# Two-layer hybrid attention encoder on one core: modulation as dot products along the free axis, and an opening in two halves of the rows

## The chip, the cores and the metric

The kernel runs on one core of a Trainium2 chip. A core has five engines with instruction queues of their own: TensorE (PE, which multiplies a 128x128 stationary operand by a moving operand of up to 512 columns), VectorE (DVE), ScalarE (ACT), GpSimd (POOL) and SyncE (SP, which here issues the transfers). They meet at semaphores. The metric is the device time of one execution in microseconds.

## The reference, cut to what matters

```python
c_act = silu(c)                                   # [1, 1024]
for i in range(2):
    mod = c_act @ ada_w[i] + ada_b[i]             # 1024 x 3072
    shift, scale, gate = split(mod, 3)
    h = rms_norm(x, norm_g[i]) * (1 + scale) + shift
    out = layer_ab(h, ...) if i == 0 else layer_diff(h, ...)
    x = x + gate * out
return rms_norm(x, final_g)

def layer_ab(h, pos, w_in, ...):
    cq, ckv, kr, q_sb, k_sb, v_sb, z = split(h @ w_in, ...)   # 384, 256, 32, 512, 512, 512, 1024
    q = rms_norm(cq, q_norm_g) @ w_uq             # rope on a part of q
    kv = rms_norm(ckv, kv_norm_g) @ w_ukv
    k_rope = rope(kr, pos)                        # one key for all heads
    ...                                           # latent attention, stick-breaking attention
    return (concat(o_mla, o_sb) * silu(z)) @ w_out
```

There are 1024 rows of 1024 features. The change touches the modulation (`mod`) and the first products of layer 0: the latents `cq` and `ckv`, the key `kr` and four of the eight blocks of `z`.

## The kernel before, in words

Every product is done in three passes (`mm3`, L172 to L175): each operand is split into a rounded part and the rest (`hi` and `lo`), and PE runs hi x hi, hi x lo and lo x hi into one bank of PSUM. A block is 128 columns of the weights; over 1024 rows and 1024 features it takes 8 x 3 matmuls of 128x512 for each half of the rows. Weights come as 0.5 MB (`w_st`); ACT rounds them (`w_hi`, L159) and POOL or DVE takes the rest (`w_lo`, L154), in `wprep`. All transfers are issued in order by SP (`dma`, L80).

The opening of layer 0 (L496 to L706) works so. All eight tiles of x are loaded, squared (ACT L526, DVE L523) and scaled by their inverse norms (`rstd_cols`, then L532 and L534). `ada_block(k)` (L538) makes the shift and scale of 128 features: `ada_st` holds 1 MB of `ada_w` with the summed index on the partitions; DVE multiplies eight pieces of 128x256 by a column of `c_act` and adds them up (L542, L544), and PE sums over the partitions with matmuls of one column (L547). PE transposes the rows (L554, two groups of four 128x128), ACT applies scale and shift (`hf`, L239) and rounds (`h0h`), and POOL or, for the first and last k, DVE takes the rest (`h0l`, L154). The three blocks of `cq` run over k, as the features come, for both halves of the rows. Then follow, each over all its k in turn (`dense_fm`): the two blocks of `ckv`, the block of `kr`, and four blocks of `z`.

Beside these stand: the rotary table `cs` (DVE L653 to L661, then the sine on ACT, L662), with a buffer of its own (tag "cs"); the rotated key, made from the banks of `kr` by a DVE multiply with `cs` (`krt`, L642), four copies on ACT (`krc`, L693) and an add on POOL; the row tables `te` and `to` (L681 to L686); and the rest of the modulation, for both gates and layer 1 (`ada_rest`, L590): two sweeps over 2048 columns, each 32 DVE operations of 128x512 (L478, L480) on 8 MB, and 16 one-column sums on PE (L487). `more(n)` hands out its steps between the blocks. Banks: `s_bank` gives three (`sc`), `d_bank` two (`psd`), `v_bank` one (`pv`), `t_bank` two (`tr`). After the opening the stick-breaking heads begin with a product into `psd`.

The order on each engine is set by a scheduler when the kernel is built, from the order of the code and from `issue_after`; at run time every engine works its queue strictly in that order.

Of the kernel before, what the change touches and what calls it, by code (L numbers as in the profile page):

```python
# [28 lines left out]
ORDER = (4, 0, 5, 1, 6, 2, 7, 3)      # by chunk parity, small beside large  # L29
ORDER_SEQ = (0, 1, 4, 2, 3, 5, 6, 7)  # first half of the tokens first  # L30
# [42 lines left out]
def kernel(ctx, tc, a, out):  # L73
# [33 lines left out]
    # scratch in DRAM  # L107
# [19 lines left out]
    # constants  # L127
# [49 lines left out]
    def dense_fm(w, rhs, evac, bank=None):  # L177
        """feature-major rows of one block of 128 columns, in two halves of the tokens"""
# [9 lines left out]
    def rstd_cols(pool, ss, n, scale, eps, name, extra=None, bufs=2):  # L188
        """(scale * ss + eps * extra) ** -0.5 of [P, n] columns"""
# [16 lines left out]
    def row_out(pool, cols, n, dst, bank):  # L206
        """[P, n] columns (query in block, block) to rows of n blocks in DRAM"""
# [6 lines left out]
    def row_bc(src, n):  # L214
        """a row in DRAM, on n partitions"""
# [5 lines left out]
    def cols_bc(dg, cols, bank):  # L221
        """four columns [P, 4] (query in block, block) as rows on every partition, in a bank"""
# [7 lines left out]
    def row_sums(tile_of, nt, bank):  # L230
        """sums over the partitions of tile_of(t), as columns [P, nt]"""
# [14 lines left out]
    def z_evac(z, func, scale):  # L246
        """z * sigmoid(z), or twice that from tanh(z / 2)"""
# [16 lines left out]
    def v_rows(vs, hi, lo, n):  # L264
        """token-major halves of the values in vs; hi(g), lo(g) of four token tiles"""
# [95 lines left out]
    def qk_dense(w, hT, b_t, bank=None):  # L361
        """[qh;qh], [ql;0], [kh;kl] of one head whose weights are [q | k]"""
# [21 lines left out]
    def par_view(ap, par, seq=False):  # L384
        """the tokens of chunks par and 2 + par; with seq of chunks 2 par and 2 par + 1"""
# [26 lines left out]
    def finish_half(pool, pv, par, e, ot, seq=False):  # L412
        """add the two halves ([vh|vl] or [vl|vh]) of a bank holding the chunks of par_view"""
# [7 lines left out]
    def load_wo(layer, half, f2s, alloc, gate, eng):  # L421
        """feature blocks 2 f2, 2 f2 + 1 of one half of the columns, times the gate, split"""
# [34 lines left out]
    def out_half(ys, wo, fs, x_, xr, bank):  # L457
        """x_ = xr + rows of y times columns of wo"""
# [35 lines left out]
    X_TAGS = [("lsq0", 1), ("lsq1", 1), ("lsq2", 1), ("zb", 2), ("zb", 2), ("lat_h", 2), ("lat_h", 2), ("lat_l", 2)]  # L494

    # =====================================================================  # L496
    # layer 0: modulation, transposed rows, latents
    # =====================================================================
    hT = [(res(f"h0h{k}"), res(f"h0l{k}")) for k in range(KC)]
    with tc.tile_pool(name="a0", bufs=1, reuse_waits="tile") as a0:  # L500
        sgc = a0.tile([P, 8], F32, name="sgc")
        nc.scalar.activation(sgc, c_sb, AF.Sigmoid)
        nc.vector.tensor_mul(c_act, c_sb, sgc)
# [10 lines left out]
        for g in range(2):  # L514
# [20 lines left out]
            if g == 0:  # L535
                ada_load(0)
# [671 lines left out]
```

## Time and profile before

| | |
|---|---|
| median of 3 runs | 1489.6 us (1489.22 to 1493.49) |
| span of the profiled execution | 1489.6 us |
| PE busy, whole span | 1394.9 us (94%) |
| DVE, ACT, POOL busy | 956.8 us (64%), 670.5 us (45%), 446.2 us (30%) |
| PE busy in the first 50 us | 6.14 us of 30, then 14.24 us of 20 |
| PE busy from 50 to 125 us | all of it |

The profiled execution is the median of the runs. A share of busy time is an average over the whole span; the opening is a small part of it, in which PE first waits for the loads, then for DVE and ACT, and from 50 us on runs almost without a gap.

### The profile page before, as it was taken

How to read it: one execution, taken by the hardware profiler on the slowest of the kernel's cores; microseconds unless marked ns; L12 is line 12 of the kernel's file. 1: busy time of each engine (PE TensorE's matmuls, PEld its weight loads, DVE VectorE, ACT ScalarE, POOL GpSimd, SP SyncE). 2: the span in 40 equal slices, each digit the busy share in tenths (PEclk: the TensorE clock that was granted, in tenths of full speed). 3: DMA queues.
4: the chain of work that ended last, by engine and by line, in shares of the span. 5: the costliest groups of instructions: out<-in, count | busy, mean ns of one | idle time of the engine just before them, and what ended most of it. 6: DMA issues, size and time to landing. Idle time of an engine off the chain costs nothing.

```text
span 1489.6 us, 20993 instructions
## 1 busy us (share of the span) xinstructions
PE 1394.9 (94%) x7328; PEld 1160.7 (78%) x7328; DVE 956.8 (64%) x2155; ACT 670.5 (45%) x1368; POOL 446.2 (30%) x509
## 2 busy tenths in 40 slices
PE   3899999999998899999879899999999999997797
PEld 2777888888886688887767688888888888886686
DVE  7769637667779865576557526665565756567674
ACT  4452145555556653555345324444444535354321
POOL 1534221132427354635133321133121222134100
PEclk9999999999999999999989999999999999999899
DMA  9269522131224166433747131324232324346262
GB/s 375 67 261 382 206 77 75 49 90 50 75 69 186 36 188 213 136 123 100 215 136 268 29 108 48 86 85 114 71 100 64 92 64 114 78 111 179 82 201 93
DMA packets 109640, 189.85 MB, mean 127 GB/s; under 512 B 8736, under 2 KB 70040, under 8 KB 107488
## 3 DMA queue, kind: packets, MB, share of 16 engines
q1 hardware_dynamic: 109536, 188.53, 39.9%
q8 instruction: 58, 0.95, 0.3%
q14 instruction: 46, 0.38, 0.1%
HBM read 131.23 MB, written 39.27 MB: 114 GB/s over the span
## 4 chain that ended last, share of the span: by engine, by line
PE 40%; DVE 5%; DMA 4%; issue 1%; POOL 1%; ACT 1%; SPq 0%; DVEq 0%; ACTq 0%; POOLq 0%
PE psd L173 8%; PE psd L175 8%; PE psd L174 8%; PE sc L294 4%; PE pv L328 3%; PE sc L173 2%; PE sc L174 2%; PE sc L175 2%; DMA y_hi<-yh_d 1%; DMA w_st<-in_wo_dram 1%; PE pv L234 1%; PE tr L308 1%; PE tr L309 1%; PE tr L310 1%; DVE g L1029 1%
## 5 line engine op out<-in xcount | busy, mean ns | idle before, releaser
L154 POOL TENSOR_TENSOR w_lo<-w_st,w_hi 128x1024 fp32r<-128x1024 f32 (+2 forms) x63 | 153.6, 2440 | 370.7 <-ACT w_hi L159 370.4
L154 DVE TENSOR_TENSOR pt_l<-tr,pt_h 128x512 fp32r<-128x512 f32 (+1 forms) x240 | 148.8, 630 | 104.9 <-ACT pt_h L159 97.4
L159 ACT CAST pt_h<-tr 128x512 fp32r<-128x512 f32 (+1 forms) x240 | 126.2, 547 | 147.0 <-PE tr L310 136.1
L175 PE MATMUL psd<-h1h,w_lo 128*128 128x512 f32 x448 | 177.0, 395 | 0.0
L174 PE MATMUL psd<-h1l,w_hi 128*128 128x512 f32 x448 | 176.2, 393 | 0.0
L173 PE MATMUL psd<-h1h,w_hi 128*128 128x512 f32 x448 | 176.1, 393 | 0.0
L294 PE MATMUL sc<-qk_k,qk_a 128*128 128x512 f32 (+2 forms) x288 | 104.8, 369 | 3.6 <-ACT g L747 1.3
L173 PE MATMUL psd<-h0h,w_hi 128*128 128x512 f32 x264 | 106.7, 404 | 0.0
L174 PE MATMUL psd<-h0l,w_hi 128*128 128x512 f32 x264 | 105.6, 400 | 0.0
L175 PE MATMUL psd<-h0h,w_lo 128*128 128x512 f32 x264 | 105.2, 398 | 0.0
L294 PE MATMUL sc<-qk_k,qk_b 128*128 128x512 f32 (+2 forms) x288 | 98.5, 349 | 0.0
L1029 DVE CUSTOM_DVE_ANT_0 g<-sc,tz 128x512 f32<-128x512 f32 (+3 forms) x128 | 72.1, 585 | 40.1 <-PE sc L294 33.7
L159 ACT CAST w_hi<-w_st 128x1024 fp32r<-128x1024 f32 x56 | 58.9, 1052 | 86.4 <-PE sc L174 36.2
L174 PEld LDWEIGHTS psd<-h1l,w_hi 128*128 128x128 f32 x448 | 84.2, 188 | 17.1
L175 PEld LDWEIGHTS psd<-h1h,w_lo 128*128 128x128 f32 x448 | 84.2, 188 | 16.1
L173 PEld LDWEIGHTS psd<-h1h,w_hi 128*128 128x128 f32 x448 | 84.2, 188 | 16.1
L328 PE MATMUL pv<-pt_l,vt 128*128 128x256 f32 x320 | 88.7, 303 | 8.2 <-DVE pt_l L154 7.4
L1035 ACT ACTIVATE g<-g,st 128x640 f32<-128x640 f32 (+3 forms) x64 | 63.4, 990 | 67.8 <-DVE st L1034 63.1
L328 PE MATMUL pv<-pt_h,vt 128*128 128x256 f32 x320 | 89.5, 296 | 3.3 <-POOL pt_h L314 1.7
L749 DVE TENSOR_TENSOR_SCAN g<-g 128x640 f32<-128x640 f32 (+3 forms) x32 | 68.7, 2148 | 14.7 <-ACT g L746 14.6
L328 PEld LDWEIGHTS pv<-pt_l,vt 128*128 128x128 f32 x320 | 62.0, 194 | 12.0 <-issue 4.7
L328 PEld LDWEIGHTS pv<-pt_h,vt 128*128 128x128 f32 x320 | 61.8, 193 | 9.5 <-DVE ot L418 2.7
(469 smaller groups left out, 3743.3 us busy)
## 6 DMA issues: line engine op xcount, KB each, us to landing
w_st<-in_w_dram SPq DMA_DIRECT2D x46, 512.0 KB
ada_st<-in_ada_k_dram SPq DMA_DIRECT2D x8, 1024.0 KB
ada_st<-in_ada_w_dram SPq DMA_DIRECT2D x16, 512.0 KB
ada_st<-in_ada_w_dram SPq DMA_DIRECT2D x8, 1024.0 KB
w_st<-in_wo_dram SPq DMA_DIRECT2D x16, 512.0 KB
yh_d<-yh SPq DMA_DIRECT2D x28, 256.0 KB
yl_d<-yl SPq DMA_DIRECT2D x28, 256.0 KB
w_st<-in_wv_dram SPq DMA_DIRECT2D x12, 512.0 KB
```

What stands on the lines that cost most here:

```text
L154: return (nc.vector if eng == "vec" else nc.gpsimd).tensor_tensor(out_, x_, y_, op=ALU.subtract)
L159: nc.scalar.copy(hi, src)
L173: mm(ps, sh, mh, start=start, stop=False)
L174: mm(ps, sh, ml, start=False, stop=False)
L175: mm(ps, sl, mh, start=False, stop=stop)
L234: mm(ps[:, t:t + 1], tile_of(t), ones, start=True, stop=True)
L294: mm(ps[:, :nn], st[:, q], mv[:, lo_:lo_ + nn], start=m == 0, stop=not diag and m == len(pairs) - 1)
L308: nc.tensor.transpose(tr[:, P:256], pb[:, (2 * j + 1) * P:(2 * j + 2) * P], identf)
L328: mm(dst, st, tt[w][:, m * 256:m * 256 + 256], start=j == 0 and m == 0 and x == 0, stop=j == n - 1 and m == 1 and x == len(ps_) - 1)
L749: nc.vector.tensor_tensor_scan(ur, ur, ur, 1.0, op0=ALU.mult, op1=ALU.bypass)
L1029: nc.vector.tensor_tensor_reduce(e_[:, sl], ps, tz[:, S - L + sl.start:S - L + sl.stop], op0=ALU.add, op1=ALU.max, scale=1.0, scalar=-3e38 ...
L1035: nc.scalar.activation(e_[:, :L], e_[:, :L], AF.Exp, scale=0.125, bias=st[:, 2 + c:3 + c], accum_out=lst[:, c1:c1 + 1] if c == 0 else st[: ...
```

## The change

- The rows are worked in two halves of 512. x tiles 0 to 3 are loaded first; x tiles 4 to 7 come after the fourth piece of `ada_w` and are normalised while the first half is multiplied. All squares are on ACT, one scaling of each half on DVE (`SC`).
- The features' scale and shift are dot products along the free axis: the pieces of `ada_w` now lie with the feature on the partition (`ada_t`, `ada_r`: prepared in this layout with the inputs), and `c`, copied to all partitions and passed through silu (`cb`), is the other operand. `dots` does two DVE operations of 128x1024 for 1 MB. Only the first 128 features are done on PE, with 16 matmuls of one column whose stationary operand is the piece of `ada_w` (`ada_0`).
- `ada_rest` uses the same dots on sixteen pieces of 1 MB; there are no sums over partitions on PE any more. The gates' row is written at the end.
- The weights of all five latent blocks (three `cq`, two `ckv`) are loaded and split at the front (`w_load`; the rest of three of them on DVE, of two on POOL), some in buffers that later hold x. The five blocks of the first half run over k in five banks; the second half follows.
- `h0l` is always made by DVE.
- Norms of the latents are added in halves (POOL, 128x512). Weights of `kr` and of the four z blocks may be fetched once the last of the eight modulation pieces is under way.
- `cb` is allocated with the tag "cs".

```diff
-WLO = ("vec", "pool")
+SC = "aava"
+WLO = ("vec", "vec", "vec", "pool", "pool")
...
+        cb = a0.tile([P, D], F32, name="cb", tag="cs")
+        dma(cb, a["c"].to_broadcast([P, D]))
+        csg = a0.tile([P, D], F32, name="csg", tag="junkd")
+        nc.scalar.activation(csg, cb, AF.Sigmoid)
+        nc.vector.tensor_mul(cb, cb, csg)
...
+            ada_st[k] = a0.tile([P, 2, D], F32, name="ada_st", tag="ld", bufs=NLD)
+            return dma(ada_st[k].rearrange("p i d -> p (i d)"), a["ada_t"][k - 1] if k else a["ada_0"])
...
+            m = a0.tile([P, 2], F32, name="adm", tag="adm", bufs=4)
+            for n in range(2):
+                junk = a0.tile([P, D], F32, name="junkd", tag="junkd")
+                nc.vector.tensor_tensor_reduce(junk, st[:, n, :], cb, op0=ALU.mult, op1=ALU.add, scale=1.0, scalar=0.0,
+                                               accum_out=m[:, n:n + 1])
+            return m
...
-            ac = a0.tile([P, 256], F32, name="ack", tag="ack", bufs=2)
-            nc.vector.tensor_scalar(ac, st[:, 0, :], c_act[:, 0:1], None, op0=ALU.mult)
-            for r in range(1, KC):
-                nc.vector.scalar_tensor_tensor(ac, st[:, r, :], c_act[:, r:r + 1], ac, op0=ALU.mult, op1=ALU.add)
-            ps = t_bank()
-            for n in range(2):
-                mm(ps[:, n:n + 1], ac[:, n * P:n * P + P], ones, start=True, stop=True)
-            nc.vector.tensor_tensor(modc[0][:, k::8], ps[:, 0:2], adab[:, k:16:8], op=ALU.add)
-            nc.vector.scalar_tensor_tensor(gsc[0][:, k:k + 1], modc[0][:, 8 + k:9 + k], 1.0, ng[:, k:k + 1],
-                                           op0=ALU.add, op1=ALU.mult)
...
+            m = dots(ada_st[k]) if k else a0_ps
+            nc.vector.tensor_tensor(modc[0][:, k::8], m, adab[:, k:16:8], op=ALU.add)
+            return nc.vector.scalar_tensor_tensor(gsc[0][:, k:k + 1], modc[0][:, 8 + k:9 + k], 1.0, ng[:, k:k + 1],
+                                                  op0=ALU.add, op1=ALU.mult)
...
+        x0 = x_load(0)
+        ada_load(0)
+        a0_ps = v_bank()[:, 0:2]
+        st0 = ada_st[0].rearrange("p i d -> p (i d)").rearrange("p (k i c) -> p k i c", i=2, c=P)
+        for n in range(2):
+            for k in range(KC):
+                mm(a0_ps[:, n:n + 1], st0[:, k, n, :], c_act[:, k:k + 1], start=k == 0, stop=k == KC - 1)
+        normed = x_norm(x0)
+        with tc.issue_after(normed.ins):
+            known = ada_block(0)
+            x_mod(0, 0, x0, "vec")
+            with tc.issue_after(known.ins):
+                for b in (0, 1):
+                    w_load(b)
+                ada_load(1)
+                for b in (2, 3):
+                    w_load(b)
+                ada_load(2)
+                w_load(4)
+        loaded = ada_load(3)
+        with tc.issue_after(loaded.ins):
+            x1 = x_load(1)
+        fb = [s_bank(), s_bank(), s_bank(), d_bank(), d_bank()]
...
+                known = ada_block(k + 1)
+                _, done = x_mod(0, k + 1, x0, "vec")
+                if k + 4 < KC:
+                    held = ada_load(k + 4)
+            if k == 2:
+                with tc.issue_after(known.ins), tc.issue_after(done.ins):
+                    x_norm(x1)
+            for b in range(5):
+                mm3(fb[b], wl[b][0][:, k, :], wl[b][1][:, k, :], hT[k][0][:, :512], hT[k][1][:, :512], k == 0, k == KC - 1)
...
+        for k in range(KC):
+            ready, _ = x_mod(1, k, x1, "vec")
+        for b in range(5):
+            latent_evac(b, 0, fb[b])
+        for b in range(5):
+            ps = (s_bank, d_bank)[b % 2]()
+            for k in range(KC):
+                mm3(ps, wl[b][0][:, k, :], wl[b][1][:, k, :], hT[k][0][:, 512:], hT[k][1][:, 512:], k == 0, k == KC - 1)
+            latent_evac(b, 1, ps)
...
+            cs = a0.tile([P, S], F32, name="cs", tag="cs")
...
+            nc.scalar.activation(cs, ar, AF.Sin, scale=cst[:, 3:4])
...
-                yield from ada_sweep(a0, src if n == 0 else lambda st, r: dma(st, a["ada_w"][1, r, 0:2048]), acc)
...
+                dst, b_ = ((gt, bias[:, 2::3, :]), (modc[1], bias[:, 3:5, :]))[n]
+                dst = dst.rearrange("p (i n) -> p i n", n=8)
+                for k in range(KC):
+                    st = a0.tile([P, 2, D], F32, name="ada_st", tag="ld", bufs=NLD)
+                    dma(st.rearrange("p i d -> p (i d)"), a["ada_r"][n, k])
+                    nc.vector.tensor_tensor(dst[:, :, k], dots(st), b_[:, :, k], op=ALU.add)
+                    yield k
...
+            part = lambda half, b: sqt[half, b // 2][:, b % 2 * 512:b % 2 * 512 + 512]
+            for half in range(2):
+                for b in range(b0 + 1, b0 + n):
+                    nc.gpsimd.tensor_tensor(part(half, b0), part(half, b0), part(half, b), op=ALU.add)
+            ss = row_sums(lambda t: part(t // 4, b0)[:, t % 4 * P:t % 4 * P + P], NT, v_bank)
...
+        with tc.issue_after(held.ins):
+            wkr = wprep(a["w0"][21])
+        dense_fm(wkr, hT, kr_evac, s_bank)
...
-            z = a0.tile([P, S], F32, name="zb", tag="zb", bufs=2)
-            dense_fm(wprep(a["w0"][8 + 4 + b]), hT, z_evac(z, AF.Sigmoid, 1.0), s_bank)
+            z = wide("zb", "a")
+            with tc.issue_after(held.ins):
+                wz = wprep(a["w0"][8 + 4 + b])
+            dense_fm(wz, hT, z_evac(z, AF.Sigmoid, 1.0), s_bank)
             dma(zs_d[b], z)
             more(4)
         more(16)
+        row_out(a0, gt, 16, gate_d.rearrange("i (n p) -> (i n) p", p=P), t_bank)
```

The order changes at three places that matter below. The first is ACT after the latents, where it makes the rotary table. Before (`lsq`, `lat_h`: squares and splits of the latents; `krc`: the copies of the rotated key; `zb`: the activation of z):

```order
L620 ACTIVATE lsq<-sc 128x512
L621 ACTIVATE lat_h<-sc,smalls 128x512
L620 ACTIVATE lsq<-sc 128x512
L621 ACTIVATE lat_h<-sc,smalls 128x512
L159 CAST w_hi<-w_st 128x1024
L620 ACTIVATE lsq<-sc 128x512
L621 ACTIVATE lat_h<-sc,smalls 128x512
L662 ACT_TABLE_LOAD
L662 ACTIVATE cs<-ar,smalls 128x1024
L159 CAST w_hi<-w_st 128x1024
L693 COPY krc<-krt 32x1024 x4
L249 ACT_TABLE_LOAD
L249 ACTIVATE zb<-sc 128x512
L159 CAST w_hi<-w_st 128x1024
L249 ACTIVATE zb<-sc 128x512 x2
```

Now:

```order
L604 ACTIVATE lat_h<-sc,smalls 128x512
L601 ACTIVATE lsq<-psd 128x512
L604 ACTIVATE lat_h<-psd,smalls 128x512
L601 ACTIVATE lsq<-sc 128x512
L604 ACTIVATE lat_h<-sc,smalls 128x512
L661 ACTIVATE rows<-tr 8x384 x3
L158 CAST w_hi<-w_st 128x1024
L637 ACT_TABLE_LOAD
L637 ACTIVATE cs<-ar,smalls 128x1024
L248 ACT_TABLE_LOAD
L248 ACTIVATE zb<-sc 128x512
L718 COPY krc<-krt 32x1024 x4
L158 CAST w_hi<-w_st 128x1024
L248 ACTIVATE zb<-sc 128x512 x2
```

The table `cs` stands behind the splits of the latents and ahead of the first `zb` and the copies in both; the weight that was rounded between the table and the copies is now rounded ahead of the table. In the changed kernel the activation that writes `cs` waits for the last reader of `cb`, whose buffer it takes; that reader is the last of the 32 dots of `ada_rest`, the second of the pair in the next listing.

The second place is DVE at the end of `ada_rest` and the rotated key. Before, where `krt` is made (`rlt`, `rlr`: steps of an inverse norm; `acc`: the sweep; `lat_l`: the rest of a latent):

```order
L622 SCALAR_TENSOR_TENSOR lat_l<-sc,smalls,lat_h 128x512
L480 SCALAR_TENSOR_TENSOR acc<-ada_st,c_act,acc 128x512
L203 SCALAR_TENSOR_TENSOR rlr<-rlt,rlr 128x8
L480 SCALAR_TENSOR_TENSOR acc<-ada_st,c_act,acc 128x512 x4
L201 TENSOR_TENSOR rlt<-rlr 128x8
L480 SCALAR_TENSOR_TENSOR acc<-ada_st,c_act,acc 128x512
L642 TENSOR_TENSOR krt<-sc,cs 128x512
L480 SCALAR_TENSOR_TENSOR acc<-ada_st,c_act,acc 128x512
L202 TENSOR_TENSOR rlt<-rlt,rlh 128x8
L642 TENSOR_TENSOR krt<-sc,cs 128x512
L203 SCALAR_TENSOR_TENSOR rlr<-rlt,rlr 128x8
L201 TENSOR_TENSOR rlt<-rlr 128x8
L202 TENSOR_TENSOR rlt<-rlt,rlh 128x8
```

Now (`junkd`, `adm`: the dots and the read of their sum; `modc`, `gsc`: shift and scale of layer 1):

```order
L675 TENSOR_TENSOR modc_121<-adm,smalls 128x2
L522 ISA junkd,adm<-ada_st,cb 128x1024
L522 ISA adm 128x1
L522 ISA junkd,adm<-ada_st,cb 128x1024
L522 ISA adm 128x1
L704 COPY te<-rqb 64x1024
L709 COPY to<-rqb 64x1024
L675 TENSOR_TENSOR modc_121<-adm,smalls 128x2
L705 TENSOR_TENSOR te<-rqb,cs 64x1024
L708 TENSOR_TENSOR to<-rqb,cs 64x1024
L697 TENSOR_TENSOR krt<-sc,cs 128x512 x2
L242 TENSOR_SCALAR gsc_123<-modc_121 128x8
L250 TENSOR_TENSOR zb<-zb,sc 128x512
```

`krt` stood in the midst of the first sweep, far ahead of the row tables `te` and `to`; it now stands behind all dots and behind both row tables.

The third is PE at the second half of the first z block, in the changed kernel (`pv`, `tr`: sums and transposes for norms and the gates):

```order
L172 MATMUL sc<-h0h_141,w_hi 128x512
L173 MATMUL sc<-h0l_142,w_hi 128x512
L174 MATMUL sc<-h0h_141,w_lo 128x512
L208 MATMUL pv<-identf,rlr 8x128
L233 MATMUL pv<-ones_sq,lsq 128x1 x8
L208 MATMUL tr<-identf,gt 16x128
L208 MATMUL pv<-identf,rlr 8x128
L172 MATMUL sc<-h0h_127,w_hi 128x512
L173 MATMUL sc<-h0l_128,w_hi 128x512
L174 MATMUL sc<-h0h_127,w_lo 128x512
```

The last three lines are the first matmuls of that half: they use the bank of `kr`'s first half, the third `sc` back, and so wait for the first `krt`. Seven of the eight halves of the z blocks, 168 matmuls of 128x512, stand behind this point. Before, the same point waited for a `krt` that followed the block of `kr`.

## Rows read from the trace of the kernel before

**Rows 1.** Two stretches: busy us of each engine, PE clock, DMA share, GB/s.

```profile
30.00:50.00 20.00, 14.24 (x60) 10.62 (x59) 19.60 (x39) 8.05 (x12) 8.14 (x6) 0.84 0.54 202
...
57.00:84.00 27.00, 27.00 (x138) 21.00 (x136) 13.89 (x30) 15.49 (x25) 7.92 (x6) 1.00 0.02 6
```

**Rows 2.** Timeline of PE, opening: start, duration, instruction, [idle before <- releaser].

```profile
33.89 1.07 PE L554 MATMUL tr<-identf,xt 128*128 128x128 f32 x8
...
45.88 0.98 PE L547 MATMUL tr<-ones_sq,ack 128*128 128x1 f32 x4 [4.54 <-DVE ack L544]
```

**Rows 3.** Timeline of PE where the rotated key meets its table.

```profile
117.62 0.39 PE L173 MATMUL sc<-h0h,w_hi 128*128 128x512 f32 x1
...
124.88 0.39 PE L175 MATMUL sc<-h0h,w_lo 128*128 128x512 f32 x1
125.64 0.50 PE L173 MATMUL sc<-h0h,w_hi 128*128 128x512 f32 x1 [0.38 <-DVE krt L642]
```

**Rows 4.** Timeline of PE at the end of the last z block.

```profile
173.87 4.07 PE L487 MATMUL tr<-ones_sq,acc 128*128 128x1 f32 x32
177.81 0.77 PE L173 MATMUL sc<-h0h,w_hi 128*128 128x512 f32 x1
...
179.23 0.63 PE L173 MATMUL psd<-h0h,w_hi 128*128 128x512 f32 x1
...
183.50 0.50 PE L174 MATMUL psd<-h0l,w_hi 128*128 128x512 f32 x1
```

**Rows 5.** DVE groups by line and form, 84 to 175 us.

```profile
L480 DVE SCALAR_TENSOR_TENSOR acc<-ada_st,c_act,acc 128x512 f32<-128x512 f32 x56 | 45.9, 872 | 0.0
L659 DVE SCALAR_TENSOR_TENSOR ar<-nred,ar 128x1024 f32<-128x1024 f32 x4 | 4.9, 1218 | 0.0
...
L622 DVE SCALAR_TENSOR_TENSOR lat_l<-sc,smalls,lat_h 128x512 fp32r<-128x512 f32 x5 | 3.7, 747 | 5.8 <-DMA cql_d<-lat_l 3.4 <-ACT lat_h L621 2.4
...
L682 DVE TENSOR_TENSOR te<-rqb,cs 64x1024 f32<-64x1024 f32 x1 | 1.2, 1223 | 0.0
...
L660 DVE TENSOR_SCALAR ar<-ar,smalls 128x1024 f32<-128x1024 f32 x1 | 0.7, 747 | 0.0
```

**Rows 6.** Timeline of ACT: first tile of x.

```profile
5.17 1.06 ACT L526 ACTIVATE junka<-xt 128x1024 f32<-128x1024 f32 x1 [2.34 <-DMA xt<-in_x_dram]
```

**Rows 7.** DMA activity of the first 60 us, in 40 equal slices.

```profile
GB/s 0 104 341 393 423 453 412 410 404 423 401 442 423 410 431 437 421 421 388 421 263 322 396 418 431 355 66 11 0 0 0 268 132 150 245 104 249 0 0 0
```

**Rows 8.** Instructions of line L523, DVE: ns min/median/max, first and last start us.

```profile
L523 DVE CUSTOM_DVE_ANT_0 junk<-xt x4: 1216/1222/1226, 6.5 to 17.5; 128x1024 f32<-128x1024 f32 x4
```

**Rows 9.** DVE groups by form, 0 to 84 us: busy us, mean ns, idle before.

```profile
L154 DVE TENSOR_TENSOR h0l<-hf,h0h 128x512 fp32r<-128x512 f32 x4 | 2.8, 688 | 3.3 <-ACT h0h L159 3.3
...
L548 DVE TENSOR_TENSOR modc<-tr,smalls 128x2 f32<-128x2 f32 x8 | 1.3, 157 | 7.4 <-PE tr L547 7.4
L154 DVE TENSOR_TENSOR w_lo<-w_st,w_hi 128x1024 fp32r<-128x1024 f32 x1 | 1.2, 1223 | 0.0
```

**Rows 10.** Timeline of POOL in the first half of the opening.

```profile
49.87 2.39 POOL L154 TENSOR_TENSOR w<-w_st,w 128x1024 fp32r<-128x1024 f32 x1 [4.81 <-ACT w L159]
52.21 2.90 POOL L154 TENSOR_TENSOR h0l<-hf,h0h 128x512 fp32r<-128x512 f32 x2
```

**Rows 11.** Timeline of DVE, one form with and without POOL beside it.

```profile
47.88 7.52 DVE L544 SCALAR_TENSOR_TENSOR ack<-ada_st,c_act,ack 128x256 f32<-128x256 f32 x7
...
55.76 3.61 DVE L544 SCALAR_TENSOR_TENSOR ack<-ada_st,c_act,ack 128x256 f32<-128x256 f32 x7
```

**Rows 12.** ACT groups by line and form, 0 to 145 us.

```profile
L239 ACT ACTIVATE hf<-tr,modc,gsc 128x512 f32<-128x512 f32 x16 | 12.2, 777 | 33.4 <-DVE gsc L549 20.9 <-PE tr L554 10.8 <-POOL h0l L154 1.7
...
L621 ACT ACTIVATE lat_h<-sc,smalls 128x512 fp32r<-128x512 f32 x7 | 4.8, 684 | 3.3 <-DMA cqh_d<-lat_h 3.3
...
L620 ACT ACTIVATE lsq<-sc 128x512 f32<-128x512 f32 x7 | 4.2, 595 | 8.6 <-PE sc L175 8.6
```

**Rows 13.** Timeline of ACT: the rotary table.

```profile
112.31 1.16 ACT L662 ACTIVATE cs<-ar,smalls 128x1024 f32<-128x1024 f32 x1
```

More of the change, by code (lines that the diff above doesn't have):

```diff
@@ L559, with dots @@
-        ada_block(0)
-        wq3 = [wprep(a["w0"][16 + b], eng_lo=WLO[b]) for b in range(2)]
-        w3 = a0.tile([P, 2, 1024], F32R, name="w3", tag="acc")
-        wq3.append(wprep(a["w0"][18], alloc=lambda name: w3[:, 0 if name == "w_hi" else 1, :]))
-        first = [[s_bank(), s_bank()], [s_bank(), d_bank()], [d_bank(), v_bank()]]
+                    last = nc.vector.tensor_scalar(xt, xt, rs[:, j:j + 1], None, op0=ALU.mult)
+            return last
+        def dots(st):
+            m = a0.tile([P, 2], F32, name="adm", tag="adm", bufs=4)
[4 more added lines that the diff above has]
+            return m
@@ L639 @@
-        krt = a0.tile([P, S], F32, name="krt", tag="lat_h", bufs=2)
-        def kr_evac(ps, half, sl):
-            nc.vector.tensor_mul(krt[:, sl], ps, cs[:, sl])
-        behind = latent(3, 16, qg, cqh_d, cql_d, rq_d, first)
+                known = ada_block(k + 1)
[5 more added lines that the diff above has]
+                    x_norm(x1)
@@ new lines, with latent_evac @@
+            for b in range(5):
+                mm3(fb[b], wl[b][0][:, k, :], wl[b][1][:, k, :], hT[k][0][:, :512], hT[k][1][:, :512], k == 0, k == KC - 1)
+        sqt = {}
+        def latent_evac(b, half, ps):
+            sl = slice(half * 512, half * 512 + 512)
+            if b % 2 == 0:
+                sqt[half, b // 2] = wide("lsq", "ab"[half])
+            gain, hi_d, lo_d, j = (qg, cqh_d, cql_d, b) if b < 3 else (kvg, ckh_d, ckl_d, b - 3)
+            nc.scalar.activation(sqt[half, b // 2][:, b % 2 * 512:b % 2 * 512 + 512], ps, AF.Square)
+            lh = a0.tile([P, 512], F32R, name="lat_h", tag="lat_h", bufs=2)
+            ll = a0.tile([P, 512], F32R, name="lat_l", tag="lat_l", bufs=2)
+            nc.scalar.activation(lh, ps, AF.Copy, scale=gain[:, j:j + 1])
+            nc.vector.scalar_tensor_tensor(ll, ps, gain[:, j:j + 1], lh.bitcast(F32), op0=ALU.mult, op1=ALU.subtract)
+            dma(hi_d[j][:, sl], lh)
+            return dma(lo_d[j][:, sl], ll)
@@ new lines, with ada_rest @@
+        dma(rel_r, rows)
+        gt = a0.tile([P, 16], F32, name="gt")
+        def ada_rest():
+            bias = adab.rearrange("p (i n) -> p i n", n=8)
+            for n in range(2):
+                dst, b_ = ((gt, bias[:, 2::3, :]), (modc[1], bias[:, 3:5, :]))[n]
[5 more added lines that the diff above has]
+                    yield k
@@ new lines, with more, latent_norm @@
+        rest = ada_rest()
+        def more(n):
+            with tc.issue_after(ready.ins):
+                for _ in range(n):
+                    next(rest, None)
+        def latent_norm(b0, n, row_d):
+            part = lambda half, b: sqt[half, b // 2][:, b % 2 * 512:b % 2 * 512 + 512]
[3 more added lines that the diff above has]
+            ss = row_sums(lambda t: part(t // 4, b0)[:, t % 4 * P:t % 4 * P + P], NT, v_bank)
+            r = rstd_cols(a0, ss, NT, 1.0 / (n * P), 1e-6, "rl")
+            row_out(a0, r, NT, row_d, v_bank)
@@ L677, with kr_evac @@
+        krt = wide("krt", "b")
+        def kr_evac(ps, half, sl):
+            nc.vector.tensor_mul(krt[:, sl], ps, cs[:, sl])
+        latent_norm(0, 3, rq_d)
+        latent_norm(3, 2, rkv_d)
+        rqb = wide("rqb", "b")
         dma(rqb, row_bc(rq_d, P))
[L678 removed]
         more(3)
[L680 removed]
+        te = wide("te", "a")
         nc.vector.tensor_copy(te[0:64], rqb[0:64])
```

175 lines of the change are left out of this document (55 added, 120 removed).

## The prediction

> **What bounds the kernel now.** Over the whole span PE is busy almost without a pause, so a change of the opening counts by how much earlier or later PE reaches the first stick-breaking head, and by nothing else. I read the stretches first: between 30 and 50 us PE has work for 14.24 of 20 us at a clock of 0.84, and DVE for 19.60; from 57 to 84 us PE is busy all 27 us while the transfers do next to nothing, a DMA share of 0.02 [rows 1]. So the start is where PE can gain, and the idle transfers from 57 us on are where loads could go. The timeline of PE says who kept it waiting there: the largest idle time, 4.54 us, ends with DVE's sweep `ack` [rows 2]. After that PE has short waits only; where the rotated key meets its table it lost 0.38 us [rows 3].
>
> As a mark I take the first product into `psd`, the first head's: 179.23 us [rows 4]. It stands behind a chain of one-column sums (32 instructions, 4.07 us), after which PE ran at the lower of its two clocks, 1.2 of 2.4 GHz, one matmul per 0.43 us, until 183.50. Ten of the head's matmuls fall into that, 2.0 us more than at the full clock, where 32 steps from 117.62 to 124.88 us give 0.227 us each [rows 3]. The changed kernel has no such chain there, so the mark to compare with is 179.2 + 2.0 = 181.2.
>
> **What the change removes.** DVE loses 64 pieces of 128x256 and the sweep of `ada_rest`, whose 56 larger steps alone took 45.9 us, 872 ns each [rows 5]. PE loses the sums over partitions; the one at 173.87 cost 4 us and the slow matmuls after it [rows 4]. This counts only if PE still bounds that stretch; below it does not. The prices that follow are worked in order of time.
>
> **First half of the rows.** SP issues in order: `c`, four tiles of x, the first piece of `ada_w`, two weights, the second piece: 5.5 MB. The first 0.5 MB of before was there at 5.17 us [rows 6], the rest comes at about 0.42 MB/us, the level of the slices from 5 to 35 us [rows 7]: 5.2 + 5/0.42 = 17.1. From there DVE has no rest until the last `h0l`: 14 dots, for which the nearest row is the 128x1024 multiply-and-sum, 1.222 us [rows 8], with the reading of its sum 1.25: 17.5. Three `w_lo` at 1.22, 3.7, eight `h0l` at 0.69, 5.5, 27 short steps at 0.16, 4.3 [rows 9], and one scaling, 0.75 [rows 5]. Together 31.8, so 48.9.
>
> Two `w_lo` on POOL run beside this, 2.4 us each [rows 10]. Seven DVE steps of one form took 7.52 us in one place and 3.61 in another [rows 11]; beside the long one POOL worked 2.39 + 2.90 = 5.29 us [rows 10]. DVE lost 3.9 us, 0.73 of POOL's time. The dots (no row shows one beside POOL) have two operands in SBUF like those steps, so I take that share, 3.5 us: 52.4. Bounds: nothing, and the whole 4.8.
>
> PE ends the half 15 matmuls later, 3.4: 55.8. Then ACT stands between the halves: five `lsq` at 0.60, three `lat_h` at 0.68, two `hf` at 0.78 [rows 12] and one rounding of 0.6 come before the second half's first operand: 7.2. PE starts again at 63.0.
>
> **Second half.** 120 matmuls at 0.227, 27.2; 28 transposes, 1.07 per eight [rows 2], 3.7; and some 2 us of half clock after the idle time, as at the end of the last z block [rows 4]. End at 96. The transposes for the last k stand 58 instructions of 136 into it, at 77; `hf`, rounding and `h0l` on top, DVE is through with the rows at 79.
>
> **The stretch that decides.** From 79 us on DVE has: the angles, four steps at 1.22 and five at about 0.7, 8.4; five `lat_l` at 0.75, 3.7 [rows 5]; 32 dots at 1.25, 40.0; 40 short steps at 0.16, 6.4. That is 58.5, so 137.5. The loads are not later: thirteen pieces and three weights, 14.5 MB, are to come from about 91 us, when the first latent weight's buffer is free; at 0.42 that is 125.5. POOL has two `w_lo`, 4.8, three adds of 128x512 at 1.45, 4.4, and a third `w_lo`, 2.4, beside it: 11.6. At 0.73 this is 8.5; a fifth to a quarter of DVE's steps there have one operand or one in PSUM, so I take 6.5: the last dot ends at 144.
>
> The bounds are nothing and the whole 11.6. The Trainium skill, page "SBUF — State Buffer", section "Who interferes with whom", has a rule that speaks against this change: a DVE operation with two SBUF operands and a GpSimd operation that reads SBUF shut each other out for the whole instruction. By that rule the upper bound would be paid here and in the first half; the trace agrees that such steps are held up, but by 0.73 of POOL's time.
>
> Only then may ACT write the rotary table, since `cb` holds its buffer: 1.16 [rows 13]; the row tables stand ahead of `krt` on DVE, 2 x 1.22 [rows 5], then `krt`, as long as an `h0l`, 0.69, and some 0.2 of handing over: 4.5. PE has meanwhile done `kr` and half a z block, 72 matmuls and some sums, to about 114, and has stood still since. It goes on at 148.5. Behind `cs` on ACT stand the z activations and the copies, but three banks leave PE two halves of lead, so they cost nothing more.
>
> **The end.** 168 matmuls at 0.227 are 38.1; the half clock at the start costs 2.8, as the 13 matmuls from 177.81 to 183.50 took 5.7 instead of 2.95 [rows 4]. The mark is at 189.4, against 181.2: 8.2 us later. The profiled execution is the median, 1489.6. **Forecast: 1498 us.**
>
> At no cost: more and other transfers on SP (each piece of `ada_rest` is one issue where the gates' were two; loads are ahead of DVE as shown), the 16 one-column matmuls for the first features (PE is idle then), the second x tiles' squares (ACT waits for gains in that stretch), the gates' row at the end (no reader before layer 0's output). If DVE were quicker, the loads at 125.5 would be late next.
>
> **Rivals.** All are decided by the end of the last dot. From 135.7 on the change loses (135.7 + 4.5 + 41 = 181.2).
>
> *POOL costs the dots nothing.* They are another instruction than those steps [rows 11], and no row shows one beside POOL. Then 3.5 and 6.5 us fall away: 1488. With part of it, anything up to 1494: no difference that can be measured, which for this kernel is 0.3%, 4.5 us. Chance 0.25.
>
> *The loads end the dots.* If DVE does its angles and latents inside waits that I count as work, and is through with the rows some us sooner, the last piece's arrival decides: 125.5 and a pair of dots, 2.5, then 4.5 and 41: 173.5, that is 7.7 us earlier, 1482. It wins where the last dot ends before 131.2. Against it: DVE's own sum is 12 us above the loads', and before it was busy 19.60 of 20 us under like work [rows 1]. Chance 0.13.
>
> *The table does not wait.* If writing `cs` were free of `cb`, PE would go on from 96 with 240 matmuls, 54.5, to 150.5: 31 us earlier, 1459. The order and the wait speak against it. Chance 0.05.
>
> *POOL shuts the dots out.* Then all of POOL's time is paid, 4.8 and 11.6 us instead of 3.5 and 6.5, which gives 6.4 more: 1504. The page named above says this; against it stands that the steps beside POOL kept a quarter of the time [rows 11]. Chance 0.13.
>
> **The numbers.** The likeliest case by itself spans 1494 to 1505. The range has to take in POOL without effect and the loads' case: from 1479 to 1506; outside lie the table that does not wait and a little at either end. The forecast has the rest, 0.44. Faster by over 0.3%: 0.13 + 0.05 = 0.18. Within 0.3%: 0.25. Slower: 0.44 + 0.13 = 0.57.
>
> **What would show it.** The dots of line L522 at 1.2 us where POOL is idle and well above beside it. PE idle for about 30 us after the first half of the first z block, released by `krt` of L697; ACT idle before the activation of L637, released by DVE; the last dot between 135 and 150 us; the first `psd` of the heads near 189. Right in the opening would be a first half that ends at 56 and a second that ends at 96. I am wrong if PE is not held there, or if the last dot ends before 131.

## The result, and the profile after

| | before | after |
|---|---|---|
| median | 1489.41 us, 4 runs (1487.08 to 1493.49) | 1508.74 us, 4 runs (1504.32 to 1514.48) |
| ratio, 95% interval | | 1.0119 [1.0084, 1.0155] |
| profiled execution: time, span | 1489.6, span 1489.6 | 1512.19, span 1510.4 |
| mark (first `psd` of the heads) | 181.2 | 193.6 |

Slower, as forecast, but by 19.3 us instead of 8.4, and 2.7 us outside the range. The mark came 12.4 us later, not 8.2; the other 8.4 us of the 20.8 between the two spans arose behind the mark.

The busy line of the profile, and two stretches of the opening (columns as in [rows 1]; the second stretch stands there too):

```profile
PE 1394.5 (92%) x7264; PEld 1163.6 (77%) x7264; DVE 937.2 (62%) x2137; ACT 679.3 (45%) x1380; POOL 421.6 (28%) x498
```

```profile
24.00:61.00 37.00, 33.27 (x138) 26.56 (x139) 28.25 (x62) 19.25 (x30) 5.56 (x2) 1.00 0.76 306
57.00:84.00 27.00, 25.30 (x125) 20.72 (x124) 11.16 (x21) 17.47 (x29) 3.76 (x3) 0.94 0.32 108
```

PE is busy as long as before (1394.5 us against 1394.9) in a longer span, so the loss is in its waits. Those of PE up to 210 us (instruction <- releaser, total, times, longest):

```profile
PE sc L172 <- DVE krt L697: 17.9, 1, 17.9
PE pv L564 <- DVE rct L200: 13.4, 1, 13.4
PE pv L208 <- DVE rlr L202: 10.0, 2, 8.6
PE pv L233 <- DVE row L210: 3.6, 1, 3.6
PE sc L173 <- DVE h0l L153: 3.5, 1, 3.5
```

All of them end with DVE. The one at `rct`, a step of x's inverse norms, belongs to the start; the largest is at `krt`, where before lost 0.38 us [rows 3]. PE in slices of 10 us:

```profile
110.00:120.00 10.00, 7.49 (x33) 5.72 (x31) 9.86 (x25) 2.34 (x2) 2.42 (x1) 1.00 1.03 428
120.00:130.00 10.00, 3.80 (x17) 3.50 (x17) 7.54 (x22) 0.00 (x0) 0.00 (x0) 0.52 0.92 379
130.00:140.00 10.00, 0.37 (x1) 0.08 (x1) 9.38 (x26) 0.00 (x0) 0.00 (x0) 0.50 0.82 299
140.00:150.00 10.00, 0.00 (x0) 0.00 (x0) 9.70 (x21) 1.51 (x2) 0.00 (x0) 0.50 0.48 200
150.00:160.00 10.00, 6.89 (x20) 5.50 (x21) 4.37 (x7) 5.69 (x6) 1.92 (x1) 0.60 0.26 107
```

Between 116.8 and 153.1 us PE stands for some 31 us in four waits (1.4, 3.6, 8.6 and 17.9), with short sums between them, while DVE is busy nearly all the time. The chain that lets it go is the one foretold; timelines of DVE, ACT and PE:

```profile
147.21 1.22 DVE L522 CUSTOM_DVE_ANT_0 junkd<-ada_st,cb 128x1024 f32<-128x1024 f32 x1
...
149.98 1.22 DVE L705 TENSOR_TENSOR te<-rqb,cs 64x1024 f32<-64x1024 f32 x1
151.24 1.22 DVE L708 TENSOR_TENSOR to<-rqb,cs 64x1024 f32<-64x1024 f32 x1
152.38 1.28 DVE L697 TENSOR_TENSOR krt<-sc,cs 128x512 f32<-128x512 f32 x2
```

```profile
148.47 1.15 ACT L637 ACTIVATE cs<-ar,smalls 128x1024 f32<-128x1024 f32 x1 [34.48 <-DVE adm L522]
```

```profile
153.11 0.80 PE L172 MATMUL sc<-h0h,w_hi 128*128 128x512 f32 x1 [17.90 <-DVE krt L697]
...
157.97 0.43 PE L174 MATMUL sc<-h0h,w_lo 128*128 128x512 f32 x1
...
193.60 0.39 PE L172 MATMUL psd<-h0h,w_hi 128*128 128x512 f32 x1
```

Against [rows 13], where the table came at 112.31, `cs` waits until 148.47 for the last dot that reads `cb`; the row tables and `krt` follow on DVE, and PE runs at one matmul per 0.43 us until 157.97.

DVE beside POOL, in the stretch that decides:

```profile
85.07 3.74 DVE L634 SCALAR_TENSOR_TENSOR ar<-nred,ar 128x1024 f32<-128x1024 f32 x3
...
89.53 2.64 DVE L634 SCALAR_TENSOR_TENSOR ar<-nred,ar 128x1024 f32<-128x1024 f32 x1
...
92.75 2.23 DVE L635 TENSOR_SCALAR ar<-ar,smalls 128x1024 f32<-128x1024 f32 x1
94.89 2.31 DVE L522 CUSTOM_DVE_ANT_0 junkd<-ada_st,cb 128x1024 f32<-128x1024 f32 x1
...
112.83 3.44 DVE L522 CUSTOM_DVE_ANT_0 junkd<-ada_st,cb 128x1024 f32<-128x1024 f32 x1
```

```profile
87.83 6.59 POOL L153 TENSOR_TENSOR w_lo<-w_st,w_hi 128x1024 fp32r<-128x1024 f32 x2 [22.42 <-ACT w_hi L158]
94.39 5.64 POOL L688 TENSOR_TENSOR lsq<-lsq 128x512 f32<-128x512 f32 x3
112.77 2.42 POOL L153 TENSOR_TENSOR w_lo<-w_st,w_hi 128x1024 fp32r<-128x1024 f32 x1 [12.74 <-ACT w_hi L158]
```

Over the lengths without POOL (1.22 for L634 and the dots, 0.75 for one operand [rows 5]) the six held steps lost 1.42, 1.48, 1.09, 0.99 (L636, 1.74 long), 0.43 (a dot of 1.65) and 2.22: 7.6 us, of POOL's 11.6. POOL's own steps took 14.65 us in these rows (6.59 + 5.64 + 2.42), some 3 us more than the 11.6: what DVE did not lose, POOL mostly lost.

### The profile page after: what moved, and what is told of

It is laid out like the page before. It is cut to its first block, busy times and chain, and to the rows that moved or that the text cites. A ratio compares the mean times of both kernels' runs of the same rounds, so it can differ in the third digit from the quotient of the medians.

```text
span 1510.4 us, 20851 instructions
## 1 busy us (share of the span) xinstructions
PE 1394.5 (92%) x7264; PEld 1163.6 (77%) x7264; DVE 937.2 (62%) x2137; ACT 679.3 (45%) x1380; POOL 421.6 (28%) x498
## 4 chain that ended last, share of the span: by engine, by line
PE 39%; DMA 5%; DVE 4%; issue 2%; POOL 2%; ACT 1%; SPq 0%; DVEq 0%; POOLq 0%; ACTq 0%
PE psd L172 8%; PE psd L173 8%; PE psd L174 8%; PE sc L293 4%; PE pv L327 4%; PE sc L172 2%; PE sc L173 2%; PE sc L174 2%; DMA rb<-rst_d 1%; DMA qk_k<-qk_a 1%; DMA w_st<-in_wo_dram 1%; PE pv L233 1%; PE tr L309 1%; PE tr L307 1%; PE tr L308 1%
## 5 line engine op out<-in xcount | busy, mean ns | idle before, releaser
L153 POOL TENSOR_TENSOR w_lo<-w_st,w_hi 128x1024 fp32r<-128x1024 f32 (+2 forms) x61 | 145.1, 2381 | 348.3 <-ACT w_hi L158 348.0
L1063 ACT ACTIVATE g<-g,st 128x640 f32<-128x640 f32 (+3 forms) x64 | 63.3, 990 | 67.4 <-DVE st L1062 62.5
L777 DVE TENSOR_TENSOR_SCAN g<-g 128x640 f32<-128x640 f32 (+3 forms) x32 | 68.8, 2149 | 14.7 <-ACT g L774 14.5
```

The lines of the kernel that those rows point to most:

```text
L153: return (nc.vector if eng == "vec" else nc.gpsimd).tensor_tensor(out_, x_, y_, op=ALU.subtract)
L777: nc.vector.tensor_tensor_scan(ur, ur, ur, 1.0, op0=ALU.mult, op1=ALU.bypass)
L1063: nc.scalar.activation(e_[:, :L], e_[:, :L], AF.Exp, scale=0.125, bias=st[:, 2 + c:3 + c], accum_out=lst[:, c1:c1 + 1] if c == 0 else st[: ...
```

## The experiments

The experiments were run in three groups: e0 to e2, then b0 to e5, then e6 to e8. "Before" was run again beside each group; its medians were 1488.96, 1490.64 and 1486.44 us, and each ratio is to the "before" of its group. The mark is the first `psd` of the heads, for the kernel before with the 2.0 us that the prediction adds. A time without an interval is one run; the marks and waits are those of one trace each.

| run | time, us | ratio [95%] | PE waits for `krt` | mark |
|---|---|---|---|---|
| e0_again | 1504.62 | 1.0097 [1.0070, 1.0124] | 17.9 | 192.8 |
| e1_cs_apart | 1499.83 | 1.0063 [1.0045, 1.0080] | 5.3 | 185.2 |
| e2_krt_first | 1480.08 | 0.9935 [0.9909, 0.9962] | 1.0 | 163.4 |
| b0_before_again | 1488.32 | | | 183.4 |
| e3_one_dot | 1502.14 | | 29.8 | 191.2 |
| e4_opening_alone | 1510.28 | | (sums 12.8) | 194.1 |
| e5_wlo_dve | 1476.29 | 0.9910 [0.9880, 0.9940] | 1.0 | 157.8 |
| e6_half_loads | 1508.98 | | 5.0 (`rlr` 19.8) | 193.3 |
| e7_half_loads_one_dot | 1495.07 | | 10.6 | 176.3 |
| e8_sums_krt_first | 1479.06 | 0.9953 [0.9935, 0.9971] | none | 164.4 |

**The changed kernel again**, unchanged.

> The changed kernel once more, unaltered, to see what its runs share after the mark (first product of the first stick-breaking head, 193.6 us in its trace, 12.4 us later than 181.2). Theory A, the wait of the rotary table is all: the shift of the mark is carried to the end, 1489.4 + 12.4 = 1502, and the 8 us more of the profiled execution (span 1510.4) are waits that differ from run to run; the mark stays within 0.5 us of 193.6 and some runs lie near 1502 to 1505. Theory B, the change also costs something fixed later on: no run below 1508, and the same places after 440 us lose time again.

The same waits and a mark 0.8 us earlier, yet 11 us less span. What differs lies behind the mark (below).

**The table in a buffer of its own.**

```
-            cs = a0.tile([P, S], F32, name="cs", tag="cs")
+            cs = a0.tile([P, 2, S], F32, name="cs", tag="acc")[:, 0, :]
```

> The rotary table gets another buffer (that of the third latent weight, free from about 92 us); nothing else is edited. Theory A, the shared buffer alone holds PE: the table is written at about 100 us, PE goes on through the z blocks from 97 us and the mark comes at about 157 us, 36 us earlier: 1466 to 1472. Theory C, the order of DVE holds it as well: krt still stands behind some 27 of the 32 dots (its place is 13 instructions after the second norm), so it comes at about 138 us, PE goes on then and the mark is at about 179 us, 14 us earlier than 193.6: 1490 to 1495.

The mark came 8.4 us earlier and not more. The wait of the table on the dots is real, but behind it stands another: `krt` came at 136.98 us, near theory C's 138, and the mark 6 us later than its 179. PE's waits from 84 us on:

```profile
PE pv L208 <- DVE rlr L202: 10.1, 2, 6.5
PE sc L172 <- DVE krt L697: 5.3, 1, 5.3
PE sc L172 <- DVE zb L250: 4.9, 1, 4.9
```

The root of the row sums (`rlr`), `krt` and the gating of the first z block (`zb`) stand behind dots in DVE's queue, `zb` behind the row tables as well; from 95 to 157 us DVE was idle for 1.2 us.

**`krt` ahead of the dots as well.** With e1's line:

```
-            with tc.issue_after(ready.ins):
+            with tc.issue_after(ready.ins), tc.issue_after(rotated[-1]):
...
+        rotated = [ready.ins]
...
-            nc.vector.tensor_mul(krt[:, sl], ps, cs[:, sl])
+            rotated.append(nc.vector.tensor_mul(krt[:, sl], ps, cs[:, sl]).ins)
```

> As the run with the table apart, and all dots but the first six are ordered behind the second krt on DVE. Theory A and C together: krt at about 115 us, PE loses 1 to 3 us there, the mark at about 156 us, 38 us earlier than 193.6 and 25 us earlier than 181.2 of before: about 1466. Theory D, the dots then become late for something after the opening (gates, layer 1), or the loads collide with those of the heads: the mark at 156, but 1475 or more at the end.

```profile
PE pv L208 <- DVE rlr L202: 1.3, 1, 1.3
PE sc L172 <- DVE krt L698: 1.0, 1, 1.0
```

All dots are still there, with the same loads, and the mark is 30 us earlier than in the changed kernel: the order did it. The expected 156 was missed by 7, and `krt` came at 121.68 instead of 115: POOL still held DVE in the opening, and behind the two short waits PE ran at 0.43 us per matmul from 122.41 to 128. The time fell by 8.9 us against before, half of what the mark gained (17.8).

**The kernel before, again**, to see the scatter.

> The kernel before once more, for a second trace. Open: whether the stretch from the mark to the end, 1308.4 us in the first trace (1489.6 - 181.2), is shorter in this kernel than the 1306.6 to 1316.8 seen in five traces of changed kernels, or varies in the same way. Theory A (it varies in both): the mark at 179.2 within 0.5 and the rest somewhere between 1303 and 1314. Theory B (the changed kernels pay something later on): 1308 or less again.

Its mark is 2.2 us later than in the first trace, its span 3.1 us shorter: what stands behind the mark varies by 5 us with nothing changed.

**One dot per piece instead of two**, in the gates' and the second layer's modulation; the second sum is left out.

```
...
-                    nc.vector.tensor_tensor(dst[:, :, k], dots(st), b_[:, :, k], op=ALU.add)
+                    nc.vector.tensor_tensor(dst[:, :, k], dots(st, 1)[:, 0:1].to_broadcast([P, 2]), b_[:, :, k], op=ALU.add)
```

> The changed kernel with one dot instead of two for each of the sixteen pieces of the rest; the second column takes the first one's sum, so half of the gates' and of layer 1's modulation is left out. All loads stay. Theory A, DVE's work ends the stretch: sixteen dots of 1.27 us less, the last dot at about 128, krt at 132.5, the mark at 173 to 174 instead of 193.6. Theory E, the loads are next behind DVE: the last piece cannot be there before 126 to 132, the last dot at 133 or later and the mark at 178 or later.

A miss: 16 dots, 20 us of DVE, gone, and the mark 2.4 us earlier. Theory E had the loads as the next limit, but at 126 to 132 us. Waits of DVE from 80 to 152 us, and its timeline:

```profile
DVE junkd L522 <- DMA ada_st<-in_ada_r_dram: 15.7, 9, 6.1
```

```profile
138.62 1.22 DVE L522 CUSTOM_DVE_ANT_0 junkd<-ada_st,cb 128x1024 f32<-128x1024 f32 x1 [6.07 <-DMA ada_st<-in_ada_r_dram]
...
145.51 1.23 DVE L522 CUSTOM_DVE_ANT_0 junkd<-ada_st,cb 128x1024 f32<-128x1024 f32 x1 [1.38 <-DMA ada_st<-in_ada_r_dram]
...
150.36 1.27 DVE L697 TENSOR_TENSOR krt<-sc,cs 128x512 f32<-128x512 f32 x2
```

The last piece lands at 145.5. In the changed kernel DVE waits for no load there, but its last dot ends at 148.4, only 3 us later. What SP waited for in this run from 110 to 136 us, and the stretch from 91 us to that landing:

```profile
SPq L79 <- DMA ada_st<-in_ada_r_dram: 12.7, 7, 2.2
```

```profile
91.00:145.50 54.50, 28.98 (x135) 21.72 (x133) 37.19 (x83) 7.33 (x12) 11.71 (x6) 0.81 0.90 350
```

SP waits for earlier pieces to land before it issues more. The DMA engines were busy 0.90 of the stretch and moved 19.1 MB (350 GB/s), in the changed kernel as well; the prediction counted 14.5 MB of loads. The issues of the changed kernel show other traffic among them:

```profile
121.29 2.38 SPq L79 DMA_DIRECT2D rel_d<-rel_r  x3
123.77 0.41 SPq L79 DMA_DIRECT2D rq_d<-row  x1
124.22 7.17 SPq L79 DMA_DIRECT2D rel_d<-rel_r  x5
131.50 3.27 SPq L79 DMA_DIRECT2D ada_st<-in_ada_r_dram  x4
```

Eight copies of the relation table stand ahead of the last four pieces. Issuing them takes SP 5.7 us (0.68 to 0.86 each); the rest of the 9.6 us it waits between them.

**The opening alone**, with before's sweep and its sums (its `ada_sweep` and `ada_cols` put back):

```
-                for k in range(KC):
-                    st = a0.tile([P, 2, D], F32, name="ada_st", tag="ld", bufs=NLD)
-                    dma(st.rearrange("p i d -> p (i d)"), a["ada_r"][n, k])
-                    nc.vector.tensor_tensor(dst[:, :, k], dots(st), b_[:, :, k], op=ALU.add)
-                    yield k
+                acc = a0.tile([P, 2048], F32, name="acc", tag="acc")
+                yield from ada_sweep(a0, src if n == 0 else lambda st, r: dma(st, a["ada_w"][1, r, 0:2048]), acc)
...
```

> The opening of the changed kernel with the rest of the modulation as before: sweeps of 128x512 and one-column sums on PE; the copied c is read for the last time in the first half, so the table does not wait. krt stands behind both sweeps in DVE's order. Theory C, whatever stands ahead of krt on DVE sets the stall: 64 sweep steps of 0.66 to 0.75 instead of 32 dots of 1.27, about 4 us more, no table and row tables between (-3.7): krt at 148 to 154, the mark at 189 to 196. Theory F, the dots are at fault and the opening alone is a gain: PE held little, the mark at 160 to 170.

As late as the changed kernel, without one dot in that stretch and with the table free of it: the dots as such are not what loses. DVE:

```profile
146.68 3.38 DVE L478 SCALAR_TENSOR_TENSOR acc<-ada_st,c_act,acc 128x512 f32<-128x512 f32 x5
149.99 1.27 DVE L720 TENSOR_TENSOR krt<-sc,cs 128x512 f32<-128x512 f32 x2
```

64 sweep steps ahead of `krt` (five in 3.38 us here) cost about what the 32 dots cost.

**e2 with all low parts of the latent weights on DVE.**

```
-WLO = ("vec", "vec", "vec", "pool", "pool")
+WLO = ("vec", "vec", "vec", "vec", "vec")
```

> As the run with krt first, and DVE takes the rest of all five latent weights, POOL of none: 2.4 us more work on DVE, but no POOL beside it between 23 and 30 us. Theory G, POOL shuts out DVE's steps there (a w_lo of 1.22 took 3.40, a step of 0.16 took 2.29): the first h0l is done at about 27 instead of 30.2, PE loses 0 to 1 us instead of 3.4 there, and all marks up to the first psd come 3 us earlier, 160.5 instead of 163.4; 1477 us. Theory H, DVE is the bound of the first half: 2.4 us more work there, the first half ends at 63 to 64 and the mark at 164 to 166.

The two steps that took 3.40 and 2.29 us beside POOL in the changed kernel (listed further below) take 1.22 and 0.15 here, with POOL idle:

```profile
24.51 1.22 DVE L153 TENSOR_TENSOR wl<-wst,wl 128x1024 fp32r<-128x1024 f32 x1
25.64 0.15 DVE L529 TENSOR_TENSOR modc<-adm,smalls 128x2 f32<-128x2 f32 x1
```

PE waits 0.3 us at the first `h0l` instead of 3.4, and the mark is another 5.6 us earlier, more than the wait and more than theory G had (160.5). What followed the wait in e2 went as well: PE ran at 0.43 us per matmul from 30.50 to 34.50 and again from 66.98 to 70 us, while in e5 it ran at 0.23 from 28.97 through the start of the second half. It is the fastest version run, 14.4 us below the kernel before of its group.

**Half the loads**, all dots (both over the half that is there), and **half the loads with one dot**; half of that modulation is left out:

```
...
-                    dma(st.rearrange("p i d -> p (i d)"), a["ada_r"][n, k])
+                    dma(st[:, 0, :], a["ada_r"][n, k][:, 0:D])
```

> The changed kernel, with half of each staged piece of the gates' and the second layer's modulation loaded and both dot products taken over that half (the other half is left out; the number of dot products is the same). If VectorE's queue alone sets PE's stall at krt: VectorE never waited for a load between 84 and 152 us in the changed kernel, so krt at 151 to 154 us and the first psd product of heads at 192 to 195 us as before. If the loads or the traffic are the limit or a large share of it (SyncE's queue, or DMA held by the relation table's stores): the mark falls by over 4 us, to under 189 us.

> Half loads and one dot product per piece (half of that modulation is left out). In the run with one dot product and full loads VectorE waited 15.7 us for staged pieces and krt came at 150.4 us. If the loads were a second limit just behind VectorE's work, both have to go for the mark to move: without the 15.7 us, krt at 133 to 137 us and the mark at 174 to 179 us. If something else held krt in that run (the table, the row sums, cs), krt stays within 3 us of 150.4 us and the mark within 3 us of 191.2 us.

Half the loads alone: mark 193.3, as the changed kernel, with `krt` at 152.24 (most of PE's wait now falls on `rlr`, ahead of it). Half the dots alone (e3): 191.2. Both:

```profile
135.91 1.27 DVE L697 TENSOR_TENSOR krt<-sc,cs 128x512 f32<-128x512 f32 x2
```

and the mark 176.3. So DVE's queue sets the stall and the loads are a second limit just behind it; of these three runs only the one that takes both away moves `krt` by more than 2 us.

**e4 with `krt` first and all low parts on DVE**, that is e5 with before's sweep and sums.

> The opening in two halves, all low parts of the latent weights on VectorE, krt ahead of the modulation in VectorE's queue, but the modulation by the sweep and the sums of the kernel before. If krt's place in VectorE's queue and the opening make the gain of the best version so far (1476 us, mark 157.8 us): mark 157 to 166 us (PE may wait up to 8 us for the first 16 sums, which now stand in the z blocks), time 1474 to 1485 us. If the dot products along the free axis make it: the mark is above 172 us and the time 1487 us or more.

The opening and the order make a gain without the dots: 16.8 us at the mark, 7.4 us in the time. Whether the dots add to it is not settled. The mark is 6.7 us behind e5's, partly by PE waiting 4.3 us at a `lat_l`; e5 gained 14.4 us against the "before" of its own group, and the intervals of the two ratios only just overlap (0.9880 to 0.9940, and 0.9935 to 0.9971).

**Behind the mark.** The stretch between the layers, 540 to 700 us after each mark, of before, before again, after and after again (e0), in this order; the eighth figure is the granted clock:

```profile
721.20:881.20 160.00, 140.64 (x664) 111.15 (x664) 80.62 (x165) 62.32 (x113) 46.23 (x42) 0.93 0.47 149
```

```profile
723.40:883.40 160.00, 141.82 (x694) 112.06 (x693) 81.89 (x166) 62.88 (x115) 47.01 (x45) 0.97 0.50 157
```

```profile
733.60:893.60 160.00, 141.56 (x668) 112.63 (x667) 82.74 (x166) 62.54 (x113) 45.19 (x45) 0.91 0.48 151
```

```profile
732.83:892.83 160.00, 140.94 (x684) 111.28 (x683) 81.67 (x166) 62.85 (x114) 45.68 (x44) 0.96 0.49 155
```

PE is idle for about as long in all four (18 to 19 us); how much of the stretch is granted at the lower clock differs. What that cost is read from the same instructions of ACT. The rounding of `yh` near the start of the stretch came at 735.04 us in after and 730.79 in e0, the activation of L1063 at its end at 894.55 and 886.37: counted from the marks, after lost 3.9 us to e0 here, of the 10.2 us that they differ behind the mark (1510.4 - 193.6 = 1316.8 against 1499.4 - 192.8 = 1306.6). Between the two executions of before the same stretch differs by 6.8 us (718.58 and 721.54, then 878.69 and 874.84).

## Why the prediction was right, and where it was wrong

**The steps that failed.** The prediction let a change of the opening count "by how much earlier or later PE reaches the first stick-breaking head, and by nothing else". What comes behind the mark was so put at nothing; it was 8.4 us in the profiled execution, and some 6.5 of the 10.7 us by which the median missed the forecast. The other step is the end of the first half, 55.8 us forecast and 61.7 measured, the main part of the 4.2 us by which the mark came later than forecast. With the second error alone the time would have been 1502, inside the range.

**Direction and mechanism held.** `cs` waits for the last dot, DVE's row tables and `krt` follow, PE stands at `krt`, and the mark is late. From the last dot on the sum is within 0.2 us: resuming 4.7 us after it (4.5 forecast), the mark 40.5 us after that (40.9).

**The opening was put to the wrong engine.** The forecast let DVE set the end of the first half and added 3.4 us: 55.8. It ended at 61.7. DVE was quick enough in sum (its last `h0l` of the half ended at 55.0), but lost its time to POOL early, in two steps:

```profile
23.96 3.40 DVE L153 TENSOR_TENSOR wl<-wst,wl 128x1024 fp32r<-128x1024 f32 x1
27.29 2.29 DVE L529 TENSOR_TENSOR modc<-adm,smalls 128x2 f32<-128x2 f32 x1
29.50 0.68 DVE L153 TENSOR_TENSOR h0l<-hf,h0h 128x512 fp32r<-128x512 f32 x1
```

```profile
30.23 0.79 PE L173 MATMUL sc<-h0l,w_hi 128*128 128x512 f32 x1 [3.45 <-DVE h0l L153]
```

Their 4.3 us over 1.22 and 0.16 are near the forecast's 3.5, but they stood ahead of the first `h0l`. From 30.2 PE had 115 of its 120 matmuls left (26.1 at 0.227), 20 transposes (2.7) and some 2 us of half clock until 34.2, and it was not idle again before the half was done: by this sum 61.0. It was worked out for the second half and left out for the first. Handing over took 4.3 us instead of 7.2, so the second half began at 66.0 (63.0), ended at 97.3 (96), and DVE was through with the rows at 81.7 (79): 2.7 us.

**The stretch that decides** took 66.7 us instead of 65: POOL cost 7.6 us, not 6.5, two short waits on PE 2.9, and the rest was a little quicker. With the 2.7 us this is the last dot at 148.4 instead of 144, and that is all of the mark's error (4.2 us). That it is no more is luck in part: the first half's 5.9 us stand against 2.9 saved in the handing over.

**POOL and the dots.** The rival in which the dots pay nothing falls with the 3.44 us dot. The Trainium skill, page "SBUF — State Buffer", section "Who interferes with whom", says that such a step and POOL's shut each other out for the whole instruction. For single steps the trace agrees: that dot lost 2.22 of POOL's 2.42 us. In sum DVE lost 0.66 of POOL's time in that stretch (7.6 of 11.6), near the 0.73 taken, and POOL's own steps took some 3 us longer meanwhile; so the rival in which DVE pays all of it was too dear.

**Rivals priced wrongly.** "The table does not wait" was to bring PE on at 96 and the mark to 150.5. Done alone (e1), it gave 185.2: with the table's wait gone, `krt` and two other short steps still stood behind dots in DVE's queue. The order listed ahead of the prediction has `krt` behind all dots, but the rival's sum left that out; e2 removed both causes and reached 163.4, e5 157.8. "The loads end the dots" had them there at 125.5; they came at 145.5 (e3). The step took 14.5 MB at 0.42 MB/us from 91 us on; 19.1 MB were moved by then, with the stores of the latents and the copies of the relation table among them, at 0.35.

**The end.** That every microsecond at the mark is one in the time did not hold. In single executions the stretch behind the mark varies: 1303.1 (before again) to 1317.0 us (e7) over the twelve traces, 10.2 us between two executions of the changed kernel. In after's profiled run it added 8.4 us; in e0's it took 1.8 away. The second median of the changed kernel, 1504.6, lies inside the range.

The medians all point one way. Against "before" and its mark at 181.2, every changed version that was run several times lost more, or gained less, in the time than at the mark: by 6.9 us (after), 4.1 (e0), 6.9 (e1), 8.9 (e2), 9.1 (e5) and 9.4 (e8); by the mark of before again, 183.4, each of these is 2.2 us larger. So the changed kernels seem to lose some microseconds behind the mark as well (ten traces: 1306.6 to 1317.0; two of before: 1303.1 and 1308.4). What loses them stays open: no run was made for it.

## What to carry to other kernels

Background work on an engine that also feeds the bottleneck costs by its place in the queue more than by its amount: with the same 32 dots the mark came 12 us later than before where they stood ahead of `krt`, and 18 us earlier where most of them stood behind it. Before pricing "remove this wait", walk the waiting instruction's own queue and ask what stands ahead of it once the wait is gone; and when removing work gives nothing, see which second limit (here the loads, 3 us behind) has taken over, and remove both together. For an opening, sum the work of each engine from its own first operand, and place a delay where it happens: 4.3 us in front of the first operand were not made up later. A gain at a mark is to be checked at the end: here about half of it arrived (e2: 17.8 us at the mark, 8.9 in the time).

## What the runs showed of the hardware

The delay beside POOL reached the smallest steps: a 128x2 addition took 2.29 us instead of 0.16 (27.29, above), and a one-operand step of 128x1024 2.23 instead of 0.75. Over the stretch that decides DVE lost 7.6 us and POOL some 3, together nearly the 11.6 us of POOL's work. The stretch between two layers differed by 3.9 and 6.8 us between two executions of one program, with PE's idle time about the same and a granted clock of 0.91 against 0.96, and 0.93 against 0.97.
